# Forming two modulation rows on VectorE in the down-projections of a two-layer step

## The chip, the cores and the metric

The kernel runs on one core of a Trainium2 chip. The metric is the device time of one execution in microseconds (us). Before the change three runs took 1547.54, 1549.52 and 1547.64 us: a median of 1547.64.

## The reference

One step of a small two-layer model on 640 tokens (512 latent, 128 context), with 1024 features. Each layer has a token mixer (neighbourhood attention in layer 0, grouped-query attention in layer 1) and then a gated feed-forward with a convolution of width three. Both stand between normalisations that are scaled, shifted and gated by six modulation rows per layer. A row is a vector of 1024 numbers, once for the latent tokens (from `c`) and once for the context tokens (from `c_ctx`): a matrix product of a single vector with a 1024x1024 part of `ada_w`.

```python
def adaln(cond, w, b):
    m = jax.nn.silu(cond) @ w + b
    return jnp.split(m[..., None, :], 6, axis=-1)

def conv_ffn(h, w_up, conv_w, conv_b, w_down):
    u = h @ w_up
    up = jnp.pad(u, ((0, 0), (1, 1), (0, 0)))
    u = up[:, :-2] * conv_w[0] + up[:, 1:-1] * conv_w[1] + up[:, 2:] * conv_w[2] + conv_b
    a, gt = jnp.split(u, 2, axis=-1)
    return (jax.nn.silu(a) * gt) @ w_down
...
    sh_as, sc_as, g_as, sh_fs, sc_fs, g_fs = adaln(c, ada_w[l], ada_b[l])
...
    xs = xs + g_as * rmsnorm(os_.reshape(bs, ts, -1) @ w_o, norm_mix_post[l])
    hs = rmsnorm(xs, norm_ffn_pre[l]) * (1.0 + sc_fs) + sh_fs
    fs = conv_ffn(hs, ffn_w_up[l], ffn_conv_w[l], ffn_conv_b[l], ffn_w_down[l])
    xs = xs + g_fs * rmsnorm(fs, norm_ffn_post[l])
```

The rows are numbered 0 to 5 in the order of `adaln`'s results: row (l, 2) is the gate of layer l's mixer, row (l, 5) the gate of its feed-forward. A gate row is kept multiplied by the gain of the normalisation that it follows.

## The kernel before

The kernel computes in float32 with matmuls in three passes: each operand is split into a high part (`wh`, `ahi`: a cast on ACT) and a low part (`wl`, `alo`: a difference on DVE or POOL). One helper (L117) records every matmul, so its rows differ only by their tiles.

**Up-projections.** `ffn` (L1155) runs for each layer. Its inner dimension of 2816 is cut into 22 chunks of 128; for each chunk seven block products (`ux`, `uy`, `uz`, 128x322 each) are formed on PE, added up and convolved on ACT and DVE (`C`, `t`, `act`), and the chunk is written to DRAM. Between these block products PE also forms modulation rows (`ada_work`). A row is 8 chunks of contraction, and a chunk four matmuls of `scolp` (the two vectors, 32 columns) with 256 columns of `ada_w` each, which are 8 instructions; several chunks stand together as one group on PE. The last chunk of a row is followed by a sum with the bias on DVE (`arow <- ada, abias`), for some rows by a second operation with the gain, and by two writes to `modrow` in DRAM from ACT's queue. Layer 0 forms five rows there, (0,5), (1,1), (1,0), (1,2), (1,4); layer 1 forms (1,5), at the places that the table `LAST` names, late in the loop.

**Down-projections.** The 640 tokens are five tiles t = 0 to 4. Group 0 holds tiles 0, 1 and 2, group 1 tiles 3 and 4. For each of the 22 chunks k a step loads 512 KB of `w_down` and the chunk's activations by SP, splits them (`load_dn`, four weight buffers), and does six matmuls 128x512 for each tile of the group. `wl` is formed on DVE for even k and on POOL for odd k. Steps 0 to 17 go through all tiles of the group; the last four steps are done tile by tile, so that tile 0 is finished while the others go on. In steps 8, 10, 12 and 14 of group 0 the first four chunks of group 1 are loaded and split ahead (`alo` 128x258 instead of 128x384). The finish of a tile (`Finish`) takes its accumulators, the gate row (`mod`) and the residual (`xo`) through DVE: `xm <- acc,mod`, `xo <- xm,ro,xo`, `xm <- xo,mod`, `xm <- xm,ro,mod`; POOL forms the small factor `ro`. In layer 0 PE then transposes `xm`, and DVE and ACT put the result into `hT`. Tile t's finish in group 0 lies beside the first steps of group 1.

The order of PE is the order of the code. On the other engines a scheduler orders the instructions by their dependences; an engine then works through its queue in that order. Loads by SP and writes from ACT's queue wait in their queues in the same way.

Of the kernel before, what the change touches and what calls it, by code (L numbers as in the profile page):

```python
# [10 lines left out]
F32 = mybir.dt.float32  # L11
# [3 lines left out]
ALU = mybir.AluOpType  # L15
# [4 lines left out]
P = 128  # L20
D = 1024
KC = D // P
# [8 lines left out]
FC = FF // P  # L31
# [30 lines left out]
TP = 1  # L62
PSN = 4
PU0 = 6
LAST = {(10, 6): 1, (8, 6): 3, (5, 6): 3, (1, 6): 3, (1, 5): 1}
HALF = (slice(0, 512), slice(512, D))
DLEAD = 3
DPRE = (8, 10, 12, 14)
# [36 lines left out]
def hybrid_step(ctx: ExitStack, tc: tile.TileContext, A, O):  # L105
    nc = tc.nc
# [9 lines left out]
    def mm(*a, **k):  # L116
        pe(nc.tensor.matmul(*a, **k))  # L117
# [10 lines left out]
    def pool(name, bufs=1, side="left", **k):  # L128
        return tc.tile_pool(name=name, bufs=bufs, side=side, reuse_waits="tile", **k)
# [5 lines left out]
    bk = Banks()  # L135
# [9 lines left out]
    def const_loads():  # L145
# [8 lines left out]
    scolp = cst.tile([P, 2 * KC + 30], F32, name="scolp")  # L154
# [119 lines left out]
    def ada_work(p, rawp, group, steps, todo, wait=1, sizes=()):  # L274

        bias = p.tile([P, 256], F32, name="abias")
        gr = p.tile([P, 256], F32, name="again")
        nc.gpsimd.memset(bias, 0.0)  # L280
        nc.gpsimd.memset(gr, 0.0)

        def quarters(row):
            return row.rearrange("(j c) -> j c", j=4)

        loads = deque((l, idx, k) for l, idx in todo for k in range(KC))
        raws = deque()
# [12 lines left out]
        for _ in range(wait):  # L300
            yield
        sizes = iter(sizes)
        while raws:
            n = min(len(raws), next(sizes, len(raws)))
            for _ in range(n):
                l, idx, k, raw = raws.popleft()
                if k == 0:
                    for q in range(2):
                        nc.sync.dma_start(bias[q::32, :], quarters(A["ada_b"][l, idx * D : idx * D + D]))
                        if idx in gain_of:  # L310
                            nc.sync.dma_start(gr[q::32, :], quarters(A[gain_of[idx]][l]))
# [7 lines left out]
                nc.vector.tensor_add(orow, ps[:, 0:256], bias)  # L319
                bk.put(ps)  # L320
                if idx in gain_of:
                    nc.vector.scalar_tensor_tensor(
                        orow, orow, 1.0 if idx in (1, 4) else 0.0, gr, op0=ALU.add, op1=ALU.mult
                    )
                for q in range(2):
                    nc.scalar.dma_start(quarters(modrow[l][idx][q]), orow[q::32, :])
            for i in range(steps):
                for _ in range(n if steps == 1 else i < n):
                    load()
                yield  # L330

    def drain(gen):
        for _ in gen:
            pass
# [817 lines left out]

    def ffn(l, hT, hT_close, xold, xnew, nxt, todo, late, late_close, side, back, first, fin0, after=None):  # L1155

        s = ExitStack()
        actd = [dr.tile([P, GAP], F32, name=f"act_{l}_{k}") for k in range(FC)]
# [25 lines left out]
        with ExitStack() as s2:  # L1184
# [196 lines left out]
            up = s2.enter_context(pool("up", 2, side))  # L1381
            if todo:
                adap = s2.enter_context(pool("ada", 1, side))
                ada = ada_work(adap, s2.enter_context(pool("adar", 3, side)), 3, *(
                    (8, todo, 4) if nxt else (3, todo, 1, (3, 2, 2, 1))))
            for p in range(PLAIN):
                conv_value(p)
                conv_gate(p)
# [1 line left out]
            for p in range(PLAIN, FC):  # L1390
                nx = p + 1 if p + 1 < FC else None
                for m, q in ((6, p), (5, p), (1, nx), (7, p), (2, nx), (3, p), (4, p)):
                    if q is None:
                        continue
                    evict(m, q, product(m, q))
                    if m == 5:
                        if nx:
                            block_sums(nx)
                        else:
                            lds.append(load_dn(len(lds), *HB[0]))  # L1400
                    elif m == 7:
# [12 lines left out]
                    if ada:  # L1414
                        for _ in range(1 if nxt else LAST.get((FC - p, m), 0)):
                            next(ada, None)
            if ada:
                drain(ada)
            store()
# [7 lines left out]
        fin = Finish(l, 5, xold, xnew, nxt, hTn, xmpool, 5, back)  # L1427
        tail, late, pre = 4, [], deque()
        dn2 = s.enter_context(pool("dn2", 4, side))
        for grp, (c0, c1) in (((0, 1, 2), HB[0]), ((3, 4), HB[1])):  # L1430
            acc = {t: [bk.get("acc") for _ in range(2)] for t in grp}

            def go(t, k, w2, hi, lo, qs=(0, 1)):
                c = (t * P if t < 4 else NS + 1) - c0
                for q in qs:
                    passes(acc[t][q], (hi[:, c : c + P], lo[:, c : c + P]),
                           tuple(x[:, 0, 512 * q : 512 * q + 512] for x in w2), k == 0, k == FC - 1)

            for k in range(FC - tail):
                if len(lds) <= k:  # L1440
                    lds.append(load_dn(k, c0, c1))
                for t in grp:
                    if t != 2 or k >= DLEAD:
                        go(t, k, *lds[k])
                if t == 2 and k == DLEAD - 1:
                    for j in range(DLEAD):
                        go(2, j, *lds[j])
                if t == 2 and k in DPRE:
                    pre.append(load_dn(len(pre), *HB[1], dn2))
                if nxt and late and k in (3, 6):  # L1450
                    late.pop(0)()
            for k in range(FC - tail, FC):
                lds.append(load_dn(k, c0, c1))
            prev, lds, pre = lds, pre, deque()
            for t in grp:
                fin.ahead(t)
                if t == 4 and not nxt:
                    for q in range(2):
                        for i in range(tail):
                            go(t, FC - tail + i, *prev[FC - tail + i], qs=(q,))  # L1460
                    fin.end(t, acc[t][0], acc[t][1], fin.stat(acc[t][0]))
                    continue
# [15 lines left out]
    def gqa_w(c0, u, own=None):  # L1478
# [2 lines left out]
    wkv = []  # L1481
    hT, hp2, late, xmp = ffn(
        0, hT, hp1.close, lambda t: xres[0][t], lambda t: xres[1][t], (1, 1, 0, NS),
        ((0, 5), (1, 1), (1, 0), (1, 2), (1, 4)), late, xmp.close, "right", "left", first, fin,
        lambda u: wkv.append(gqa_w(1024, u)),
    )

# [474 lines left out]
```

## Time and profile before

| | |
|---|---|
| median of three runs | 1547.64 us |
| profiled execution, span of the trace | 1546.0 us |
| PE busy | 1512.8 us |
| DVE, ACT, POOL busy | 1024.1, 854.2, 701.8 us |
| group 0 of layer 0's down-projection | 664.6 to about 755 us |
| group 0 of layer 1's down-projection | 1388.0 to about 1478 us |

Times in rows of the profile are microseconds from the start of the span. A row of a timeline gives start, duration, engine, line, operation, the tile written and the tiles read, their shapes, a count of equal instructions in a row, and in brackets how long the engine was idle ahead of it and what ended that. An instruction's printed time includes the time in which it is held back after its start. A row of a group gives the total busy time and the mean of one in ns. Idle time of an engine costs nothing unless another waits for it, in the end PE.

### The profile page before, as it was taken

To read this page: it belongs to the slowest core of one execution; us is meant where nothing else is said; L and a number is where in the kernel's file an instruction comes from. 1 tells how busy PE (TensorE), PEld (TensorE's weight loads), DVE (VectorE), ACT (ScalarE), POOL (GpSimd) and SP (SyncE) were. 2 spreads that over 40 slices of the span, in tenths; PEclk is the share of its full clock that TensorE was granted. 3 is DMA by queue.
4 is the path that set the end of the run, shared out by engine and by line. 5 is a ranking of instruction groups with operands and counts; after the bars stand their busy time and mean duration, and the time that the engine had idled before them with its cause. 6 is when DMAs were issued, how large, how long until landed. Compare 5 with 4: busy or idle time off the path is not lost.

```text
span 1546.0 us, 26097 instructions
## 1 busy us (share of the span) xinstructions
PE 1512.8 (98%) x9709; PEld 1344.4 (87%) x9709; DVE 1024.1 (66%) x1648; ACT 854.2 (55%) x1624; POOL 701.8 (45%) x606
## 2 busy tenths in 40 slices
PE   6999999999999999999999999999999999999998
PEld 5988998888999999978887878878899999988886
DVE  4553453659877666756757877773988887786554
ACT  5665564646655555654544447763666655554443
POOL 1554463432355455525444464532235666542433
PEclk9999999999999999999999999999999999999999
DMA  9745454253565665388574421015433334447664
GB/s 318 210 122 159 122 132 116 64 190 124 183 224 177 221 190 162 114 277 272 178 234 155 129 69 42 2 40 190 153 114 115 119 111 156 132 164 252 226 221 131
DMA packets 196666, 243.99 MB, mean 158 GB/s; under 512 B 11484, under 2 KB 153020, under 8 KB 196540
## 3 DMA queue, kind: packets, MB, share of 16 engines
q1 hardware_dynamic: 186704, 235.74, 47.7%
q10 hardware_dynamic: 9836, 6.59, 2.5%
q8 instruction: 76, 1.25, 0.3%
q14 instruction: 50, 0.41, 0.1%
HBM read 214.38 MB, written 26.34 MB: 156 GB/s over the span
## 4 chain that ended last, share of the span: by engine, by line
PE 66%; DVE 5%; ACT 2%; issue 2%; POOL 1%; DMA 1%; POOLq 0%; DVEq 0%; ACTq 0%
PE acc L117 19%; PE ux L117 18%; PE uz L117 8%; PE gp L117 5%; PE uy L117 4%; PE po L117 3%; PE y L117 3%; PE s L117 2%; PE tp L120 2%; PE ada L117 1%; DMA wr<-in_ffn_w_up 1%; DVE t L1281 1%; ACT gp L1692 1%; PE tr L120 0%; DVE xo L400 0%
## 5 line engine op out<-in xcount | busy, mean ns | idle before, releaser
L180 POOL TENSOR_TENSOR wl<-wr,wh 128x1024 fp32r<-128x1024 f32 x70 | 173.3, 2480 | 238.5 <-ACT wh L178 223.5
L1204 POOL TENSOR_TENSOR wl<-wr,wh 128x1024 fp32r<-128x1024 f32 x76 | 183.5, 2435 | 46.9 <-ACT wh L1203 43.3
L117 PE MATMUL ux<-B,wh 128*128 128x322 f32 x832 | 200.1, 311 | 0.9 <-ACT u L1258 0.9
L1281 DVE SCALAR_TENSOR_TENSOR t<-C,cw,t 128x644 f32<-128x644 f32 x176 | 156.3, 888 | 51.3 <-ACT t L1279 50.7
L117 PE MATMUL acc<-wh,alo 128*128 128x512 f32 x440 | 172.3, 392 | 0.3 <-DVE alo L1173 0.3
L178 ACT CAST wh<-wr 128x1024 fp32r<-128x1024 f32 x140 | 145.6, 1048 | 48.5 <-DMA wr<-in_ffn_w_down 37.4
L117 PE MATMUL acc<-wh,ahi 128*128 128x512 f32 x440 | 171.9, 391 | 0.0
L117 PE MATMUL acc<-wl,ahi 128*128 128x512 f32 x440 | 171.8, 391 | 0.0
L117 PE MATMUL uz<-B,wh 128*128 128x322 f32 x640 | 156.2, 312 | 0.9 <-ACT v L1258 0.9
L117 PEld LDWEIGHTS ux<-B,wh 128*128 128x128 f32 x832 | 143.6, 189 | 3.4 <-issue 1.2
L1173 DVE TENSOR_TENSOR alo<-ain,ahi 128x384 fp32r<-128x384 f32 (+1 forms) x88 | 84.0, 973 | 84.9 <-ACT ahi L1171 84.0
L117 PE MATMUL ux<-B,wl 128*128 128x322 f32 x416 | 129.5, 311 | 2.7 <-DVE wl L1204 2.7
L117 PE MATMUL qk<-hT,wh 128*128 128x384 f32 (+1 forms) x512 | 122.4, 315 | 0.0
L117 PEld LDWEIGHTS uz<-B,wh 128*128 128x128 f32 x640 | 110.9, 189 | 4.3 <-ACT v L1258 1.5
L1204 POOL TENSOR_TENSOR vl<-wr,vh 128x1024 fp32r<-128x1024 f32 x38 | 96.3, 2535 | 24.6 <-ACT vh L1203 24.3
L1203 ACT CAST wh<-wr 128x1024 fp32r<-128x1024 f32 x84 | 84.8, 1049 | 40.8 <-DVE wr L1227 40.5
L1279 ACT ACTIVATE t<-C,cw 128x644 f32<-128x644 f32 x88 | 78.6, 893 | 47.8 <-DVE C L1309 40.3
L180 DVE TENSOR_TENSOR wl<-wr,wh 128x1024 fp32r<-128x1024 f32 x70 | 91.3, 1315 | 20.1 <-ACT wh L178 19.5
L117 PE MATMUL uz<-B,wl 128*128 128x322 f32 x320 | 99.6, 311 | 0.3 <-POOL wl L1204 0.3
L117 PEld LDWEIGHTS acc<-wh,alo 128*128 128x128 f32 x440 | 82.5, 188 | 18.8 <-DVE alo L1173 1.1
L117 PEld LDWEIGHTS acc<-wl,ahi 128*128 128x128 f32 x440 | 82.6, 188 | 17.9
L117 PEld LDWEIGHTS acc<-wh,ahi 128*128 128x128 f32 x440 | 82.6, 188 | 17.8
(259 smaller groups left out, 3857.7 us busy)
## 6 DMA issues: line engine op xcount, KB each, us to landing
wr<-in_ffn_w_up SPq DMA_DIRECT2D x88, 512.0 KB
wr<-in_ffn_w_down SPq DMA_DIRECT2D x88, 512.0 KB
wr<-in_ada_w SPq DMA_DIRECT2D x72, 512.0 KB
act<-act SPq DMA_DIRECT2D x44, 321.0 KB
wr<-in_na_w_qkv SPq DMA_DIRECT2D x24, 512.0 KB
mod<-modrow SPq DMA_DIRECT2D x20, 512.0 KB
ain<-act SPq DMA_DIRECT2D x44, 192.0 KB
wf<-in_ada_w SPq DMA_DIRECT2D x16, 512.0 KB
```

The lines of the kernel that those rows point to most:

```text
L117: pe(nc.tensor.matmul(*a, **k))
L120: pe(nc.tensor.transpose(*a, **k))
L178: i = nc.scalar.copy(hi, raw)
L180: j = (low or nc.vector).tensor_sub(lo, raw, f32(hi))
L1173: pin(nc.vector.tensor_sub(lo[:, 0 : c1 - c0], ain[:, 0 : c1 - c0], f32(hi[:, 0 : c1 - c0])))
L1203: nc.scalar.copy(hl[0], src)
L1204: low.tensor_sub(hl[1], src, f32(hl[0]))
L1279: nc.scalar.activation(t, taps(0), AF.Identity, bias=cw[:, 3, n : n + 1], scale=cw[:, 1, n : n + 1])
L1281: nc.vector.scalar_tensor_tensor(t, taps(d), cw[:, w, n : n + 1], t, op0=ALU.mult, op1=ALU.add)
L1692: nc.scalar.activation(self.pt[i].rearrange("p (a b) -> p a b", a=2), sv, AF.Exp, bias=nm, scale=-1.0, accum_out=su)
```

## The change

Row (1,2) is no longer formed in layer 0's up-projections, nor row (1,5) in layer 1's, and `LAST` is gone. Layer 1's up-projections hold no modulation work now. A new generator, `ada_vec`, forms the two rows in the down-projections. It takes a row in two halves of 512 columns, and a half in eight units, one for each chunk of contraction. A unit is a load of 256 KB by SP into one of three buffers and two DVE operations 128x512, one for each of the two vectors: a product (`TENSOR_SCALAR`) for the first unit, `raw * scolp + acc` (`SCALAR_TENSOR_TENSOR`) for the others. One step after the eighth unit PE sums `acc` over the partitions: eight matmuls with a column of ones (`one`, 32x128 each, 16 instructions). DVE adds the bias and multiplies by the gain, and ACT's queue writes the half to `modrow`. Layer 1 does a unit in each step of its down-projection, so both halves fall into group 0 (sums over partitions behind steps 8 and 16). Layer 0 does one in each second step: the first half in group 0, the second in group 1.

```diff
+    def ada_vec(p, todo, lag=1):
+        one = p.tile([P, 2, 32], F32, name="one")
...
+        units = deque((l, idx, half, k) for l, idx in todo for half in range(2) for k in range(KC))
...
+                raw = p.tile([P, 512], F32, tag="wr", name="wr", bufs=3)
+                nc.sync.dma_start(raw, A["ada_w"][l, k * P : k * P + P, c0 : c0 + 512])
...
+            if k == 0:
+                acc = p.tile([P, 2, 512], F32, tag="acc", name="acc")
+                for q in range(2):
+                    nc.sync.dma_start(bias[q::32, :], pieces(A["ada_b"][l, idx * D : idx * D + D], half))
+                    if idx in gain_of:
+                        nc.sync.dma_start(gr[q::32, :], pieces(A[gain_of[idx]][l], half))
+            for q in range(2):
+                col = scolp[:, 2 * k + q : 2 * k + q + 1]
+                if k == 0:
+                    nc.vector.tensor_scalar(acc[:, q], raw, col, None, op0=ALU.mult)
+                else:
+                    nc.vector.scalar_tensor_tensor(acc[:, q], raw, col, acc[:, q], op0=ALU.mult, op1=ALU.add)
+            load()
...
+            for _ in range(lag):
+                yield
+            ps = bk.get("ada")
+            for q in range(2):
+                for j in range(4):
+                    mm(ps[32 * j : 32 * j + 32, 0:P], one[:, q], acc[:, q, j * P : j * P + P], start=q == 0, stop=q == 1)
+            nc.vector.tensor_add(bias, ps[:, 0:P], bias)
...
+            for q in range(2):
+                nc.scalar.dma_start(pieces(modrow[l][idx][q], half), bias[q::32, :])
...
-                ada = ada_work(adap, s2.enter_context(pool("adar", 3, side)), 3, *(
-                    (8, todo, 4) if nxt else (3, todo, 1, (3, 2, 2, 1))))
+                ada = ada_work(adap, s2.enter_context(pool("adar", 3, side)), 3, 8, todo, 4)
...
+        vec = ada_vec(s.enter_context(pool("adv", 1, side)), todo_dn)
+        next(vec)
...
+                if not nxt or k % 2:
+                    next(vec, None)
+            if not nxt or t == 4:
+                drain(vec)
...
-        ((0, 5), (1, 1), (1, 0), (1, 2), (1, 4)), late, xmp.close, "right", "left", first, fin,
+        ((0, 5), (1, 1), (1, 0), (1, 4)), ((1, 2),), late, xmp.close, "right", "left", first, fin,
...
-        1, hT, r_h3.close, lambda t: xres[2][t], y_out, None, ((1, 5),), late, xmp.close, "left", "right", first, fin
+        1, hT, r_h3.close, lambda t: xres[2][t], y_out, None, (), ((1, 5),), late, xmp.close, "left", "right", first, fin
```

Line numbers of the changed kernel are 62 higher in `ffn` (L1173 is L1235), and its weight halves stand at L179. PE's order differs only by the groups taken out (in layer 0's up-projections one of 12 matmuls becomes 8, two of 12 and one of 4 go; in layer 1's one of 12, two of 8 and one of 4) and the four groups of eight put in.

DVE at the end of layer 1's up-projection and the start of its down-projection, before:

```order
L1281 SCALAR_TENSOR_TENSOR t<-C,cw_79,t 128x2x322 x4
L319 TENSOR_TENSOR arow<-ada,abias 128x256
L1292 TENSOR_TENSOR act<-t,sl 128x644
L322 SCALAR_TENSOR_TENSOR arow<-arow,again 128x256
L1307 TENSOR_TENSOR C<-ux,v_15534 128x322
L180 TENSOR_TENSOR wl<-wr,wh 128x1024
L1309 TENSOR_TENSOR C<-uz,u_15511 128x322
L1281 SCALAR_TENSOR_TENSOR t<-C,cw_79,t 128x2x322 x2
L1173 TENSOR_TENSOR alo<-ain,ahi 128x384 x3
L1281 SCALAR_TENSOR_TENSOR t<-C,cw_79,t 128x2x322 x2
L1292 TENSOR_TENSOR act<-t,sl 128x644
```

and from the same place in the changed kernel, some rows on (`wl` and the first `alo` are of the first steps):

```order
L1371 TENSOR_TENSOR C<-uz,u_15514 128x322
L1343 SCALAR_TENSOR_TENSOR t<-C,cw_79,t 128x2x322 x2
L1235 TENSOR_TENSOR alo<-ain,ahi 128x384 x2
L372 TENSOR_SCALAR acc<-wr,scolp 128x512 x2
L374 SCALAR_TENSOR_TENSOR acc<-wr,scolp,acc 128x512
L1343 SCALAR_TENSOR_TENSOR t<-C,cw_79,t 128x2x322
L374 SCALAR_TENSOR_TENSOR acc<-wr,scolp,acc 128x512
L1343 SCALAR_TENSOR_TENSOR t<-C,cw_79,t 128x2x322
L374 SCALAR_TENSOR_TENSOR acc<-wr,scolp,acc 128x512
L1354 TENSOR_TENSOR act<-t,sl 128x644
L374 SCALAR_TENSOR_TENSOR acc<-wr,scolp,acc 128x512
L1235 TENSOR_TENSOR alo<-ain,ahi 128x384
```

The two `arow` operations ahead of `C <- ux` are gone, and the units of the moved row stand among the last convolution work and the following `alo`.

DVE in layer 0 where group 0's tile 2 is finished beside group 1's steps 4 to 8, before (`wl` and `alo` at the end are step 8's):

```order
L387 TENSOR_TENSOR xm<-acc,mod 128x512
L389 TENSOR_TENSOR xm<-acc,mod 128x512
L1173 TENSOR_TENSOR alo<-ain,ahi 128x258
L400 SCALAR_TENSOR_TENSOR xo<-xm,ro,xo 128x512 x2
L412 TENSOR_TENSOR xm<-xo,mod 128x512 x2
L419 SCALAR_TENSOR_TENSOR xm<-xm,ro,mod 128x512 x2
L456 TENSOR_TENSOR hT_7811<-tr,hT_7810 128x4x128 x2
L1173 TENSOR_TENSOR alo<-ain,ahi 128x258
L180 TENSOR_TENSOR wl<-wr,wh 128x1024
```

and now:

```order
L451 TENSOR_TENSOR xm<-acc,mod 128x512
L462 SCALAR_TENSOR_TENSOR xo<-xm,ro,xo 128x512 x2
L474 TENSOR_TENSOR xm<-xo,mod 128x512 x2
L481 SCALAR_TENSOR_TENSOR xm<-xm,ro,mod 128x512 x2
L374 SCALAR_TENSOR_TENSOR acc<-wr,scolp,acc 128x512 x5
L518 TENSOR_TENSOR hT_7753<-tr,hT_7752 128x4x128 x2
L374 SCALAR_TENSOR_TENSOR acc<-wr,scolp,acc 128x512 x2
L1235 TENSOR_TENSOR alo<-ain,ahi 128x258
L374 SCALAR_TENSOR_TENSOR acc<-wr,scolp,acc 128x512
L179 TENSOR_TENSOR wl<-wr,wh 128x1024
```

Eight sums of the second half stand between the last operation on tile 2 and step 8's `wl`. The other units of that half (two products and six sums, behind the bias and gain of the first half) stand ahead of tile 0's `xm <- acc,mod`, and the last operation on tile 1 (L481) now stands ahead of step 4's `wl` instead of behind it.

SP in layer 1, the loads around steps 14 and 15 of group 0 (`ain` is the activations, `wr` of `in_ffn_w_down` the weights, 128x258 a preload for group 1), in the changed kernel:

```order
L1231 DMA ain<-act_14_12500 128x384
L173 DMA wr<-in_ffn_w_down 128x1024
L368 DMA again<-in_norm_ffn_post 4x128 x2
L355 DMA wr<-in_ada_w 128x512
L366 DMA abias<-in_ada_b 4x128 x2
L355 DMA wr<-in_ada_w 128x512 x2
L1231 DMA ain<-act_3_12489 128x258
L173 DMA wr<-in_ffn_w_down 128x1024
L355 DMA wr<-in_ada_w 128x512 x2
L1231 DMA ain<-act_15_12501 128x384
```

Before, only `ain` and `wr` of `in_ffn_w_down` alternated there. A unit's load waits until DVE has used the buffer, and the loads behind it in SP's queue wait with it. The load of the gate row for the finish (`mod <- modrow_5`) stood at the start of group 0 and now stands behind the weights of group 1's step 5.

More of the change, by code (lines that the diff above doesn't have):

```diff
@@ L64 @@
 PU0 = 6
-LAST = {(10, 6): 1, (8, 6): 3, (5, 6): 3, (1, 6): 3, (1, 5): 1}
 HALF = (slice(0, 512), slice(512, D))
@@ L330, in ada_work, with pieces, load @@
                 yield
+    def ada_vec(p, todo, lag=1):
+        one = p.tile([P, 2, 32], F32, name="one")
+        nc.gpsimd.memset(one, 0.0)
+        for q in range(2):
+            nc.gpsimd.memset(one[:, q, q : q + 1], 1.0)
+        bias = p.tile([P, P], F32, name="abias")
+        gr = p.tile([P, P], F32, name="again")
+        nc.gpsimd.memset(bias, 0.0)
+        nc.gpsimd.memset(gr, 0.0)
+        def pieces(row, half):
+            return row[512 * half : 512 * half + 512].rearrange("(j c) -> j c", j=4)
+        units = deque((l, idx, half, k) for l, idx in todo for half in range(2) for k in range(KC))
+        raws = deque()
+        def load():
+            if units:
+                l, idx, half, k = units.popleft()
+                c0 = idx * D + 512 * half
+                raw = p.tile([P, 512], F32, tag="wr", name="wr", bufs=3)
+                nc.sync.dma_start(raw, A["ada_w"][l, k * P : k * P + P, c0 : c0 + 512])
+                raws.append((l, idx, half, k, raw))
+        for _ in range(3):
+            load()
+        yield
+        while raws:
+            l, idx, half, k, raw = raws.popleft()
+            if k == 0:
[10 more added lines that the diff above has]
+                    nc.vector.scalar_tensor_tensor(acc[:, q], raw, col, acc[:, q], op0=ALU.mult, op1=ALU.add)
+            load()
+            if k < KC - 1:
+                yield
+                continue
+            for _ in range(lag):
+                yield
+            ps = bk.get("ada")
[3 more added lines that the diff above has]
+            nc.vector.tensor_add(bias, ps[:, 0:P], bias)
+            bk.put(ps)
+            if idx in gain_of:
+                nc.vector.scalar_tensor_tensor(
+                    bias, bias, 1.0 if idx in (1, 4) else 0.0, gr, op0=ALU.add, op1=ALU.mult
+                )
+            for q in range(2):
+                nc.scalar.dma_start(pieces(modrow[l][idx][q], half), bias[q::32, :])
@@ L1150, in hybrid_step, with ffn @@
     r_na.close()
-    def ffn(l, hT, hT_close, xold, xnew, nxt, todo, late, late_close, side, back, first, fin0, after=None):
+    def ffn(l, hT, hT_close, xold, xnew, nxt, todo, todo_dn, late, late_close, side, back, first, fin0, after=None):
         s = ExitStack()
@@ L1414, in ffn @@
                     if ada:
-                        for _ in range(1 if nxt else LAST.get((FC - p, m), 0)):
-                            next(ada, None)
+                        next(ada, None)
             if ada:
```

## The prediction

> **What bounds the kernel now.** I read the page first: the engines' busy shares, the chain that ended last, and the clock.
>
> ```profile
> span 1546.0 us, 26097 instructions
> ...
> PE 1512.8 (98%) x9709; PEld 1344.4 (87%) x9709; DVE 1024.1 (66%) x1648; ACT 854.2 (55%) x1624; POOL 701.8 (45%) x606
> ...
> PEclk9999999999999999999999999999999999999999
> ...
> PE 66%; DVE 5%; ACT 2%; issue 2%; POOL 1%; DMA 1%; POOLq 0%; DVEq 0%; ACTq 0%
> ```
>
> PE is busy for 98% of the span, at full granted clock in every slice, and it makes up 66% of the chain. So a microsecond of PE work taken out is a microsecond gained, as long as nothing behind PE becomes late, and a microsecond that DVE makes PE wait is lost. The question is one of exchange: PE time in the up-projections against DVE time in the down-projections. What PE spends on a modulation group stands in the timeline of layer 1's up-projection (start, duration, instruction, count):
>
> ```profile
> 1286.69 0.31 PE L117 MATMUL ux<-B,wl 128*128 128x322 f32 x1
> 1286.84 0.31 PE L117 MATMUL ux<-B,wh 128*128 128x322 f32 x1
> 1287.07 1.50 PE L117 MATMUL ada<-wr,scolp 128*32 128x256 f32 x24
> 1288.51 0.41 PE L117 MATMUL uz<-B,wh 128*128 128x322 f32 x1
> 1288.76 0.31 PE L117 MATMUL uz<-B,wl 128*128 128x322 f32 x1
> ...
> 1380.00 0.64 PE L117 MATMUL ada<-wr,scolp 128*32 128x256 f32 x8
> ```
>
> Block matmuls start 0.15 us apart (1286.69, 1286.84). From 1286.84 to 1288.76 would be 0.30 without the group and is 1.92, so 24 instructions cost **1.62 us**, 0.12 more than their printed 1.50. With the same 0.12, 8 cost 0.76; each instruction is (1.50 - 0.64)/16 = 0.054, so 16 cost 1.62 - 8 x 0.054 = 1.19.
>
> **What the change takes away.** A row is 64 PE instructions. Layer 1's row stands as 24, 16, 16 and 8: 1.62 + 1.19 + 1.19 + 0.76 = **-4.76**. In layer 0 the order of PE loses two groups of 24, one of 8, and 8 instructions of another: 1.62 + 1.62 + 0.76 + 8 x 0.054 = **-4.43**.
>
> At the end of layer 1's up-projection DVE and ACT lose work as well, first DVE:
>
> ```profile
> 1384.19 0.42 DVE L319 TENSOR_TENSOR arow<-ada,abias 128x256 f32<-128x256 f32 x1
> 1384.52 0.82 DVE L1292 TENSOR_TENSOR act<-t,sl 128x644 f32<-128x644 f32 x1
> 1385.26 0.41 DVE L322 SCALAR_TENSOR_TENSOR arow<-arow,again 128x256 f32<-128x256 f32 x1
> 1385.59 0.48 DVE L1307 TENSOR_TENSOR C<-ux,v 128x322 f32<-128x322 f32 x1
> ```
>
> and next to it on PE, then on ACT:
>
> ```profile
> 1386.13 0.42 PE L117 MATMUL ux<-B,ah 128*128 128x322 f32 x1 [1.23 <-DVE C L1307]
> ```
>
> ```profile
> 1386.78 0.51 ACT L1171 CAST ahi<-ain 128x384 fp32r<-128x384 f32 x1 [3.02 <-DMA modrow<-arow]
> ```
>
> PE waits 1.23 us there for C, which stood behind both row operations. Without them C is about 2 x 0.33 us earlier (starts 1385.26 to 1385.59). The next activations of ACT stood behind a wait of 3.02 us for the row's write, and with it goes a short wait of PE for the second step's operands. What is late next is DVE's own queue of convolution work, so I take **-1.0**, between 0 and -1.4. The row that now ends layer 0's up-projection ends as before, so nothing goes there.
>
> **What it adds on PE.** Four groups of 16 matmul instructions with half the columns (32x128). No row shows that shape. If time follows columns they take 0.33 + 16 x 0.027 = 0.76, if it follows instructions 1.19; I take 0.8, nearest to the columns that the 322 and 512 wide rows follow: **+3.2** (3.0 to 4.8). The POOL memsets and the small loads of bias and gain lie in idle time: POOL waited 8.56 us before its first weight half of the down-projection.
>
> ```profile
> 1388.38 2.41 POOL L180 TENSOR_TENSOR wl<-wr,wh 128x1024 fp32r<-128x1024 f32 x1 [8.56 <-ACT wh L178]
> ```
>
> **What it adds on DVE.** Per row 28 three-operand sums and 4 products of 128x512. The nearest rows by form:
>
> ```profile
> L400 DVE SCALAR_TENSOR_TENSOR xo<-xm,ro,xo 128x512 f32<-128x512 f32 x40 | 28.4, 746 | 4.8 <-POOL ro L379 3.9 <-DMA xo<-in_x_sample 0.8
> L597 DVE TENSOR_SCALAR xT<-xT,gcol,hcol 128x512 f32<-128x512 f32 x8 | 4.3, 543 | 2.1 <-ACT hT L596 2.0
> ```
>
> The same sum takes 0.75 alone and 1.41 for two in a row (771.01 below), the product 0.54. A unit is 1.4 us, a row about 22 us of DVE. DVE can afford that on average; what counts is where it stands.
>
> **Layer 0, group 1.** The order puts six sums and two products ahead of the finish of tile 0, and eight sums between the last operation of tile 2 (771.01) and the weight half of step 8 (773.88).
>
> ```profile
> 744.30 0.69 DVE L387 TENSOR_TENSOR xm<-acc,mod 128x512 f32<-128x512 f32 x1 [4.60 <-ACT junk L370]
> ...
> 756.83 5.69 DVE L419 SCALAR_TENSOR_TENSOR xm<-xm,ro,mod 128x512 f32<-128x512 f32 x2 [1.08 <-POOL ro L379]
> ...
> 771.01 1.41 DVE L419 SCALAR_TENSOR_TENSOR xm<-xm,ro,mod 128x512 f32<-128x512 f32 x2 [1.09 <-POOL ro L379]
> ...
> 773.88 1.22 DVE L180 TENSOR_TENSOR wl<-wr,wh 128x1024 fp32r<-128x1024 f32 x1
> 775.01 2.96 DVE L1173 TENSOR_TENSOR alo<-ain,ahi 128x258 fp32r<-128x258 f32 x2
> ```
>
> and on POOL, then on PE, at the same times:
>
> ```profile
> 756.76 5.21 POOL L180 TENSOR_TENSOR wl<-wr,wh 128x1024 fp32r<-128x1024 f32 x2
> ...
> 774.75 2.60 POOL L180 TENSOR_TENSOR wl<-wr,wh 128x1024 fp32r<-128x1024 f32 x1 [3.78 <-ACT wh L178]
> ```
>
> ```profile
> 779.77 0.40 PE L117 MATMUL acc<-wh,ahi 128*128 128x512 f32 x1
> 780.00 0.39 PE L117 MATMUL acc<-wl,ahi 128*128 128x512 f32 x1
> ```
>
> The first part (6 x 0.7 + 2 x 0.54 = 5.3 us) mostly fills the 4.60 us idle; the load for its third unit is issued late, and DVE's wait of 1.08 ahead of 756.83 takes up part of that, so tile 2 comes about 1 us late (0 to 2.5). The second part adds 8 x 0.67 = 5.4. And POOL's own half (774.75) now falls among these sums: where two such operations meet, one waits for the other. Two sums took 5.69 us at 756.83 instead of 1.41 while POOL worked from 756.76 to 761.97, and two alo took 2.96 at 775.01 instead of 0.8. So one block more, 2.3. Against that stands the slack: the half of step 8 ends at 775.1, and PE uses it at 780.00, or 0.8 later for the ones ahead: 5.7. Stall: 1 + 5.4 + 2.3 - 5.7 = **+3.0**, between 0 (no block, no lateness) and 6.3 (a second block and the full lateness).
>
> A rule bears on the block. The Trainium skill, "SBUF — State Buffer", section "Who interferes with whom", says that a DVE instruction with two SBUF inputs and a GpSimd instruction that reads SBUF share a port as an exclusive lock: the second waits for the whole of the first. It speaks against this change, as every added sum has two SBUF inputs. The rows at 756.83 and 775.01 agree. By it the term is 3.0 as above; without it the block of 2.3 would go and 0.7 remain.
>
> **Layer 1, group 0.** Here there is a unit in every step. A step is 18 matmuls 0.23 us apart (779.77 to 780.00): 4.1 us. Two steps, 8.2 us, hold on DVE two alo, one weight half and now four sums, and one weight half on POOL:
>
> ```profile
> 1410.94 0.55 DVE L1173 TENSOR_TENSOR alo<-ain,ahi 128x384 fp32r<-128x384 f32 x1
> ```
>
> The busy table by stretch (PE, PEld, DVE, ACT, POOL busy, clock, DMA share, GB/s) has for 20 us of it:
>
> ```profile
> 1400.00:1420.00 20.00, 20.00 (x90) 16.57 (x89) 13.29 (x13) 11.68 (x18) 7.81 (x4) 1.00 0.80 266
> ```
>
> For two steps that is 1.1 + 1.2 + 2.8 = 5.1 on DVE, blocked once by POOL's 2.4: 7.5 of 8.2. The 13.29 that DVE shows now hold blocked time too. The preloads for group 1 add four short alo, two halves on each engine: 1.6 + 2.4 + 4.8 = 8.8 us. Eight steps that hold them need 4 x 7.5 + 8.8 = 38.8 us of 32.9 if nothing overlaps: 5.9 too much, which a lead of 3 to 6 us over PE from the steps ahead has to cover. I take **+1.5**, between 0 and 5.9. Layer 0's group 0 has a unit in every second step: 0 (to 1).
>
> **Sum.** -4.76 - 4.43 - 1.0 + 3.2 + 3.0 + 1.5 = -2.5. From the span of 1546.0 this gives 1543.5. The runs' median of 1547.64 is 1.64 above that span; with this it is **1545.2**.
>
> **Rivals.** *The stalls vanish* (the leads are enough): -4.76 - 4.43 - 1.0 + 3.2 + about 1 = -6.0, **1541.6**. For it: DVE is at 66%, and buffers run ahead. Against it: eight sums in one piece ahead of a weight half.
>
> *DVE and POOL become the bound* (the slower side): neither stretch has the lead, so layer 0 pays 6.3 and layer 1 5.9: -10.2 + 3.2 + 12.2 = +5.2, **1552.9**. It decides against the change once the two stalls together pass 7.0 + 3.1 us. For it: the rows above, where DVE and POOL exclude each other. Against it: DVE was idle for 4.60 us ahead of 744.30, and for 1.1 twice after.
>
> *Loads become the bound in layer 1*. A unit of 0.26 MB in 4.1 us is 64 GB/s more, 330 where 266 stood at a share of 0.80, so about 1.0 of the engines; SP issues unit loads that wait for DVE with weight loads queued behind them.
>
> ```profile
> 1426.53 1.05 ACT L178 CAST wh<-wr 128x1024 fp32r<-128x1024 f32 x1 [6.53 <-DMA wr<-in_ffn_w_down]
> ```
>
> Casts already wait for weights. From 1400 to 1420 the free share is 0.20 x 20 = 4.0 us, and five units, 1.3 MB at 266/0.80 = 333 GB/s, need 3.9; if bursts leave half of it unused, 2 us are missing, on top of the 1.5: **1547.2**, and the weights behind that queue late.
>
> *The removal gives less than it says*: the groups covered waits for evictions or weights, and PE now waits for those instead. Half of 9.2 lost: **1549.8**. Against it: no wait is printed behind the groups above.
>
> *Layer 1's gate row is late*: its last sums end with step 16, and tile 0's finish reads it back after step 17 and four tail steps of six matmuls, 4.1 + 5.5 = 9.6 us later. The chain is two DVE operations (0.8), a write (3.02, the wait of ACT above) and a read, taken as long: about 7 us, and what stands ahead of it in the queues. 2 us late gives **1547.2**.
>
> **How the numbers follow.** 0.2% is about what a measurement of this kernel can tell from no change: 3.1 us, 1544.5 to 1550.7. Chances: forecast 0.36 (own range 1543.5 to 1548), stalls vanish 0.27, DVE and POOL bound 0.15, loads 0.12, less removed 0.06, late gate row 0.04. Faster: 0.27 and a quarter of the forecast, 0.36. Slower: 0.15 and small parts of loads and removal, 0.19. Same: 0.45. The range for 8 in 10 reaches from 1540.8, near the sum without stalls, to 1551.5, into the case of the bound; beyond it lie the lowest of the first and the half of the second.
>
> **What will show it.** The up-projections should lose the groups named, PE's wait of 1.23 at 1386 should be shorter, and ones groups of about 0.65 printed should stand in four places. Layer 0's step 8 should show PE waiting 1 to 6 us for wl or alo. In layer 1 PE's waits up to step 17 should sum to under 6 us, named DVE if the lock is right, DMA if the loads are. No wait in step 8 of layer 0, or single waits above 5 us elsewhere, make this wrong.

## The result and the profile after

The changed kernel took 1559.53 us (median of 5 runs, 1558.4 to 1560.91) against 1547.64 us: a ratio of 1.0076, 95% interval 1.0065 to 1.0087. It is **slower by 11.9 us** (0.8%), outside the range of 1540.8 to 1551.5 that was forecast. The profiled run has a span of 1556.6 us, 10.6 more than before. Its page:

```profile
span 1556.6 us, 26097 instructions
...
PE 1512.1 (97%) x9645; PEld 1343.5 (86%) x9645; DVE 1077.7 (69%) x1716; ACT 853.5 (55%) x1624; POOL 705.5 (45%) x614
...
PE 35%; DVE 4%; ACT 2%; DMA 2%; issue 2%; POOL 1%; SPq 0%; DVEq 0%; POOLq 0%; ACTq 0%
```

PE's share of the last chain fell from 66% to 35%: at some point the chain now leaves PE. PE's busy time hardly fell, although 64 instructions net are gone; that will matter below. What PE waited for, from the view of waits (engine, tile and line, releaser: total us, times, longest):

```profile
PE acc L116 <- DVE wl L179: 3.8, 1, 3.8
...
PE acc L116 <- DVE act L1354: 3.3, 2, 1.6
...
PE acc L116 <- POOL wl L179: 2.4, 2, 1.5
...
PE tr L119 <- DVE hT L518: 1.2, 1, 1.2
```

None of the four stood in the profile before. To see how much each stage gained or lost, the same PE instruction is looked up in both timelines: a matmul at the start of each down-projection, and the first long wait of the stage after layer 0's. Before:

```profile
668.19 0.50 PE L117 MATMUL acc<-wh,alo 128*128 128x512 f32 x1 [0.27 <-DVE alo L1173]
...
824.39 0.73 PE L117 MATMUL gp<-wl,hT 128*128 128x512 f32 x2 [0.39 <-DVE wl L180]
...
1391.41 0.50 PE L117 MATMUL acc<-wh,alo 128*128 128x512 f32 x1
```

and after:

```profile
662.98 0.50 PE L116 MATMUL acc<-wh,alo 128*128 128x512 f32 x1 [0.27 <-DVE alo L1235]
...
831.33 0.73 PE L116 MATMUL gp<-wl,hT 128*128 128x512 f32 x2 [0.41 <-DVE wl L179]
...
1395.39 0.50 PE L116 MATMUL acc<-wh,alo 128*128 128x512 f32 x1 [0.27 <-DVE alo L1235]
```

Up to layer 0's down-projection the changed kernel is 5.2 us ahead, of which 0.7 is the wait for the first load of the program (7.4 us against 8.1). At the end of that down-projection it is 6.9 behind: **12.1 us lost there**. Up to layer 1's down-projection it catches up to 4.0 behind, a gain of 3.0; layer 1's mixer, which did not change, takes about 0.5 of that stretch's gain. At the end it is 10.6 behind: **6.6 lost** in layer 1's down-projection.

Where the 12.1 went: PE at step 8 of layer 0's group 1 shows the largest part.

```profile
779.27 0.40 PE L116 MATMUL acc<-wh,ahi 128*128 128x512 f32 x1
783.47 0.80 PE L116 MATMUL acc<-wl,ahi 128*128 128x512 f32 x1 [3.80 <-DVE wl L179]
784.06 0.63 PE L116 MATMUL acc<-wh,alo 128*128 128x512 f32 x1
...
788.75 0.58 PE L116 MATMUL acc<-wl,ahi 128*128 128x512 f32 x1
789.17 0.39 PE L116 MATMUL acc<-wh,alo 128*128 128x512 f32 x1
```

After the wait of 3.80 us the matmuls start 0.43 us apart instead of 0.23, up to 788.75. The busy table of these 10 us shows why:

```profile
780.00:790.00 10.00, 6.53 (x17) 5.16 (x18) 8.59 (x13) 2.81 (x4) 2.37 (x1) 0.66 0.59 197
```

The granted clock, the share of its full clock that PE was given, is 0.66 over this stretch (third number from the end). The page, whose slices are 39 us long, shows 9 in every one. From 783.47 to 789.17 thirteen matmuls take 5.70 us where 13 x 0.233 = 3.03 would do: **2.7 us on top of the wait**. Slow matmuls count as busy, and that is one reason why PE's busy time hardly fell; the groups of ones are another. The Trainium skill, "TensorE: Matmul & The Clock Gate", "Part 1: The HAM clock gate", says that TensorE falls to half clock after an idle window of about 3.4 us and comes back after a busy one. The wait of 3.80 us here agrees; runs below show a fall behind shorter waits too.

The DVE queue ahead of that half, and POOL beside it:

```profile
771.88 1.42 DVE L481 SCALAR_TENSOR_TENSOR xm<-xm,ro,mod 128x512 f32<-128x512 f32 x2 [1.09 <-POOL ro L441]
773.22 5.54 DVE L374 SCALAR_TENSOR_TENSOR acc<-wr,scolp,acc 128x512 f32<-128x512 f32 x5
778.68 1.27 DVE L518 TENSOR_TENSOR hT<-tr,hT 128x512 fp32r<-128x512 f32 x2
779.88 1.39 DVE L374 SCALAR_TENSOR_TENSOR acc<-wr,scolp,acc 128x512 f32<-128x512 f32 x2
781.20 0.41 DVE L1235 TENSOR_TENSOR alo<-ain,ahi 128x258 fp32r<-128x258 f32 x1
781.54 0.73 DVE L374 SCALAR_TENSOR_TENSOR acc<-wr,scolp,acc 128x512 f32<-128x512 f32 x1
782.20 1.21 DVE L179 TENSOR_TENSOR wl<-wr,wh 128x1024 fp32r<-128x1024 f32 x1
```

```profile
774.26 2.62 POOL L179 TENSOR_TENSOR wl<-wr,wh 128x1024 fp32r<-128x1024 f32 x1 [2.41 <-ACT wh L177]
```

Tile 2 is 0.87 us late (771.88 against 771.01), the eight sums stand where the order has them, and five of them take 5.54 us instead of 3.4 while POOL forms its half. All eight take 5.54 + 1.39 + 0.73 = 7.66 us; the prediction had 5.4 + 2.3. What it had differently is the place of PE. It let PE come 0.8 us later, for the ones. PE came 0.5 us earlier than before (779.27 against 779.77 for the matmul ahead of the wait), because the gain of the up-projections was not yet used up. That is 1.3 us less slack, and more than the whole difference between 3.0 and 3.80.

What it did not have is the wait for `act`. DVE at the start of layer 0's down-projection:

```profile
664.72 0.89 DVE L372 TENSOR_SCALAR acc<-wr,scolp 128x512 f32<-128x512 f32 x2 [1.32 <-DMA wr<-in_ada_w]
665.52 0.55 DVE L1235 TENSOR_TENSOR alo<-ain,ahi 128x384 fp32r<-128x384 f32 x1
665.99 0.88 DVE L1343 SCALAR_TENSOR_TENSOR t<-C,cw,t 128x644 f32<-128x644 f32 x1
666.78 0.74 DVE L374 SCALAR_TENSOR_TENSOR acc<-wr,scolp,acc 128x512 f32<-128x512 f32 x1
667.44 0.88 DVE L1343 SCALAR_TENSOR_TENSOR t<-C,cw,t 128x644 f32<-128x644 f32 x1
668.24 0.74 DVE L374 SCALAR_TENSOR_TENSOR acc<-wr,scolp,acc 128x512 f32<-128x512 f32 x1
668.90 0.82 DVE L1354 TENSOR_TENSOR act<-t,sl 128x644 f32<-128x644 f32 x1
```

The first product waits 1.32 us at the head of the queue for its load, and two sums stand ahead of the last `act`. `act` reads `t`, which lies in PSUM, the memory of PE's accumulators, and tile 2's accumulators take its place there. So PE waits for it at the first matmul of tile 2, 1.61 us in layer 0 and 1.65 in layer 1:

```profile
669.87 0.47 PE L116 MATMUL acc<-wh,ahi 128*128 128x512 f32 x1 [1.61 <-DVE act L1354]
```

POOL has no part in this wait. Its last work ahead of it ends at 661.99, and its next half comes behind it:

```profile
674.20 2.73 POOL L179 TENSOR_TENSOR wl<-wr,wh 128x1024 fp32r<-128x1024 f32 x1 [12.21 <-ACT wh L177]
```

So layer 0's 12.1 are the waits of 1.61, 1.25 and 3.80, 2.7 of slow clock and two groups of ones (0.78 each, below), 10.9. Layer 1's 6.6 are waits of 1.65, 0.88 and 1.49 and two groups of ones, 5.6. Part of the 2.2 left over lies around the waits: the three matmuls at 667.87, 669.87 and 670.18 take 2.31 us from the first start to the last instead of 0.46, so the wait printed as 1.61 costs 1.85.

### The profile page after: what moved, and what is told of

The parts are those of the page before. It is cut to its first block, busy times and chain, and to the rows that moved or that the text cites. A ratio compares the mean times of both kernels' runs of the same rounds, so it can differ in the third digit from the quotient of the medians.

```text
span 1556.6 us, 26097 instructions
## 1 busy us (share of the span) xinstructions
PE 1512.1 (97%) x9645; PEld 1343.5 (86%) x9645; DVE 1077.7 (69%) x1716; ACT 853.5 (55%) x1624; POOL 705.5 (45%) x614
## 3 DMA queue, kind: packets, MB, share of 16 engines
q8 instruction: 76, 1.25, 0.3%
## 5 line engine op out<-in xcount | busy, mean ns | idle before, releaser
L179 POOL TENSOR_TENSOR wl<-wr,wh 128x1024 fp32r<-128x1024 f32 x70 | 174.5, 2496 | 250.8 <-ACT wh L177 246.0
L1235 DVE TENSOR_TENSOR alo<-ain,ahi 128x258 fp32r<-128x258 f32 (+1 forms) x88 | 74.8, 867 | 61.5 <-ACT ahi L1233 55.7
L1265 ACT CAST wh<-wr 128x1024 fp32r<-128x1024 f32 x84 | 84.7, 1049 | 46.5 <-DVE wr L1289 46.2
L1233 ACT CAST ahi<-ain 128x258 fp32r<-128x258 f32 (+1 forms) x88 | 39.5, 460 | 120.8 <-PE acc L116 79.7
L179 DVE TENSOR_TENSOR wl<-wr,wh 128x1024 fp32r<-128x1024 f32 x70 | 92.7, 1335 | 15.7 <-ACT wh L177 15.1
```

Of the source, the lines that this page charges most:

```text
L179: j = (low or nc.vector).tensor_sub(lo, raw, f32(hi))
L1233: pin(nc.scalar.copy(hi[:, 0 : c1 - c0], ain[:, 0 : c1 - c0]))
L1235: pin(nc.vector.tensor_sub(lo[:, 0 : c1 - c0], ain[:, 0 : c1 - c0], f32(hi[:, 0 : c1 - c0])))
L1265: nc.scalar.copy(hl[0], src)
```

## The experiments

Three theories stood open. **Place**: sums push back a few DVE operations that PE waits for. **Loads**: the extra loads crowd the DMA engines and SP. **Throughput or lock**: DVE and POOL together have too much to do, because they exclude each other, so that one stands still while the other works. The runs of one group share runs of the kernel before on the same chip (1548.0 to 1548.5 us); ratios are to those.

**One row at a time, and parts left out.** Layer 0's row alone, with layer 1's back in its up-projection:

```diff
-        1, hT, r_h3.close, ..., None, (), ((1, 5),), late, ...
+        1, hT, r_h3.close, ..., None, ((1, 5),), (), late, ...
```

> Only layer 0's row (1,2) is moved; layer 1's row (1,5) is formed in its up-projection as before. Place theory (the sums push back DVE operations that PE waits for, act ahead of tile 2's accumulators and the weight half of step 8, and PE then runs at half clock for some us): layer 0 gives 4.4 us and loses 12, so about 7.5 us slower than before, 1555. Load theory (the extra loads crowd the DMA engines and SP's queue): layer 0 adds its loads at half the rate of layer 1 and should carry less than half of the 11.9 us lost, so 1550 or less.

Measured 1556.47, ratio 1.0065 (1.0047 to 1.0083): 8.5 us slower. The waits are 1.37, 1.25 and 3.79 us at the same places, and the clock falls again. The smaller load rate costs more, which speaks against loads. In its profiled run, the slowest of the four (1561.38 us), layer 1 waited 2.73 us for a POOL half though nothing is added there. So layer 1 has little to spare even without the added sums, in this execution at least.

Layer 1's row alone:

```diff
-        ((0, 5), (1, 1), (1, 0), (1, 4)), ((1, 2),), late, ...
+        ((0, 5), (1, 1), (1, 0), (1, 2), (1, 4)), (), late, ...
```

> Only layer 1's row (1,5) is moved. Place theory: its up-projection gives about 3.9 us, its down-projection loses 7 (tile 2's start 2, two weight halves of POOL 3.4, two ones groups 1.5), so 3 us slower than before, 1550.7. Load theory: the larger part of the 11.9 us, 1554 or more.

Measured 1549.22, ratio 1.0006 (0.9996 to 1.0015): no difference that can be told, against 3 us expected from the place theory and 6 or more from loads. Its waits in layer 1 are the one for `act` (1.18) and four of 0.2 to 0.5. Both rows apart cost 8.5 + 1.2 = 9.7 us, near the 11.9 of both together.

DVE's operations cut to 8 of 512 columns, everything else kept:

```diff
-    nc.vector.scalar_tensor_tensor(acc[:, q], raw, col, acc[:, q], op0=ALU.mult, op1=ALU.add)
+    nc.vector.scalar_tensor_tensor(acc[:, q, 0:8], raw[:, 0:8], col, acc[:, q, 0:8], op0=ALU.mult, op1=ALU.add)
```

> Both rows moved with all their loads and sums over partitions, but the operations on VectorE work on 8 of 512 columns, so the two rows are wrong. Place theory: the waits in both down-projections are gone, the time is 8.3 us below before plus 3 us for the ones groups plus about 1 for what is left, 1543. Load theory: the waits stay, 1555 or more.

Measured 1542.85, ratio 0.9967 (0.9956 to 0.9978): every wait that the change brought into the two down-projections is gone. Loads, groups of ones and writes are all still there. **The loads by themselves cost nothing; the loss comes with DVE's sums.**

The rows not formed at all; of `ada_vec` only the writes are left, and they write zeros:

```diff
-            for q in range(2):
-                col = scolp[:, 2 * k + q : 2 * k + q + 1]
...
+                for q in range(2):
+                    nc.scalar.dma_start(pieces(modrow[l][idx][q], half), bias[q::32, :])
```

> The two rows are not formed at all: no loads, no sums, no ones groups, only the writes of zeros to the rows' place. This is what the removal gives by itself. The prediction's terms: 4.76 + 4.43 + 1.0 = 10.2 us, 1537.4. Cover theory (in layer 1 the groups taken out covered waits of PE for ACT's evictions, of which the changed kernel shows 0.95 and 0.72 us): about 8.3 us, 1539.3.

Measured 1541.06, ratio 0.996 (0.9945 to 0.9975): taking the rows out of the up-projections gives 7.0 us (3.9 to 8.5 by the interval), not the 10.2 of the prediction; the 8.3 of the cover theory is still within. Layer 1's PE shows where some of it stays:

```profile
1370.57 0.41 PE L116 MATMUL uz<-B,wl 128*128 128x322 f32 x1 [0.56 <-POOL wl L1238]
...
1373.41 0.41 PE L116 MATMUL ux<-B,wh 128*128 128x322 f32 x1 [0.96 <-ACT u L1292]
...
1376.20 0.42 PE L116 MATMUL uz<-B,wh 128*128 128x322 f32 x1 [0.73 <-ACT v L1292]
```

The wait of 1.23 for `C` is gone, and three of 2.25 together stand in its place: the last modulation group covered them, in part. Instead of -1.0 the transition is +0.8 (2.25 less the 1.23 and 0.20 that stood there before). The changed kernel shows the same three places, with 0.44, 0.94 and 0.72: +0.7.

**Moving the sums.** First unit held behind the last `act`, by an order without a wait:

```diff
+        marks["hold"] = marks["act"]
...
+                if marks.get("hold"):
+                    behind(i, marks["hold"])
```

> The changed kernel with the first unit's product held behind the last act operation of the up-projection on VectorE (an order without a wait, in both layers). Place theory: act is no longer late, tile 2's accumulators are free in time, and the waits of 1.61 and 1.64 us at step 2 of both down-projections go: 1559.5 - 3.3 = 1556. Throughput theory (VectorE and GpSimd together have too much to do, wherever it stands): the same work is only later, the waits come back at the following weight halves: 1559.

Measured 1555.79, ratio 1.0052 (1.0038 to 1.0065), as the place theory has it in time, but not quite in its parts: both waits for `act` are gone, while layer 1 now waits 3.34 us once for a DVE half instead of 0.88 and 1.49 for POOL's. There the throughput theory is right. The profiled run is the slowest of its four (1558.16 us); it also pays for a slow clock in layer 0's up-projection, shown in the last section.

The last four units of layer 0's row held behind the low parts of steps 9 to 15:

```diff
+                marks["hold"] = marks["alo"] if nxt and grp[0] == 3 and k >= 9 else None
-                if not nxt or k % 2:
+                if not nxt or (k % 2 and (grp[0] == 0 or k != 7)):
```

> The changed kernel with the last four units of layer 0's row held behind the activations' low part of steps 9, 11, 13 and 15 of group 1, so that the eight sums no longer stand ahead of step 8's weight half. Place theory: the wait of 3.80 us goes, and with it the half clock that follows it (6.8 us at half speed, 3.4 us): 1559.5 - 7.2 = 1552. Throughput theory: the wait moves to steps 10 to 16 and most of the loss stays, 1557 or more.

Measured 1551.3, ratio 1.0021 (1.0012 to 1.003): 8.2 us less than the changed kernel. The wait at step 8 is gone, and the clock stays at full speed.

Only the last two units held back:

```diff
+                marks["hold"] = marks["alo"] if nxt and grp[0] == 3 and k >= 11 else None
```

> The changed kernel with only the last two units of layer 0's row held back (four sums instead of eight ahead of step 8's weight half). Dose test of the half clock: the wait should shrink by 4 x 0.68 = 2.7 us to about 1.1 us. If the half clock follows only a long wait (it followed 2.73 and 3.80 us, and none of the waits up to 1.65), it goes too: 1559.5 - 2.7 - 3.4 = 1553.4. If it follows any wait at this place: 1556.8.

Measured 1553.76, ratio 1.0034 (1.0021 to 1.0048). The wait at step 8 is 1.13 us, and the matmuls behind it keep their pace:

```profile
782.86 0.50 PE L116 MATMUL acc<-wl,ahi 128*128 128x512 f32 x1 [1.13 <-DVE wl L179]
783.20 0.40 PE L116 MATMUL acc<-wh,alo 128*128 128x512 f32 x1
```

2.7 us less of waiting gave 5.8 us by the medians: behind the short wait the price of the slow clock is not paid.

Both holds:

> Both holds of the two runs above together. Place theory: 1559.5 - 3.3 - 7.2 = 1549, about level with before (1548.0), and what is left against the run without rows (1541.1) is four ones groups (3.0), layer 1's late weight halves (2 to 3) and layer 0's transposes (1 to 2). Throughput theory: 1556 or more.

Measured 1549.37, ratio 1.0006 (0.9997 to 1.0015): level with before, with the loss at step 8 and at `act` gone. What is left is mainly a wait of 2.38 us in layer 1 (the clock is 0.83 over those 10 us) and 1.26 ahead of layer 0's transposes. DVE and POOL ahead of the first:

```profile
1433.53 10.50 DVE L376 SCALAR_TENSOR_TENSOR acc<-wr,scolp,acc 128x512 f32<-128x512 f32 x6
```

```profile
1431.36 7.33 POOL L179 TENSOR_TENSOR wl<-wr,wh 128x1024 fp32r<-128x1024 f32 x2 [5.98 <-ACT wh L177]
1440.15 2.68 POOL L179 TENSOR_TENSOR wl<-wr,wh 128x1024 fp32r<-128x1024 f32 x1 [1.46 <-ACT wh L177]
```

Six sums that need 4.0 us take 10.50, and the first two halves of POOL, which need 4.8, take 7.33. The two engines take turns. Looked at one by one, three of the six sums take 2.88 to 2.90 us and three 0.73 or 0.74, one long sum for each of the three halves. So a half on POOL costs DVE about 2.2 us of standing still, more than the 1.2 it needs to form the half itself.

**Taking POOL out of the pair.** All weight halves of the down-projections on DVE:

```diff
-            w2 = wsplit(rows(w_dn, k, 1, 0, D), 1, D, nc.gpsimd if k % 2 else None, own)
+            w2 = wsplit(rows(w_dn, k, 1, 0, D), 1, D, None, own)
```

With both holds:

> The run with both holds, and the weight halves of odd steps of the down-projections formed on VectorE instead of GpSimd. Lock theory (two operations of 128x1024 and 128x512 on GpSimd and VectorE with two inputs in SBUF exclude each other, so a half on GpSimd costs VectorE about 2.3 us of standing still, more than the 1.22 us of doing it itself): the wait of 2.38 us in layer 1 and its 1.7 us of half clock and the 1.26 us ahead of layer 0's transposes go: 1549.4 - 5 = 1544.5, faster than before (1548.5). Load theory of VectorE (no lock, its queue is simply full): 1.22 us more in every second step, 1553 or more.

Measured 1542.06, ratio 0.9963 (0.995 to 0.9975): 7.3 us less than with the holds alone, and no wait of PE in either down-projection. The kernel before with this edit alone:

> The kernel before with the same one edit: odd weight halves of the down-projections on VectorE. PE waits nowhere there on them, so by both theories nothing changes: 1548 to 1549. If it is faster by 2 us or more, the gain of the run with both holds is not the lock's beside the sums.

Measured 1546.88, ratio 0.9995 (0.9986 to 1.0004): nothing, although there too DVE stands still less (its `alo` groups take 46.2 us instead of 84.2). PE waited on none of it. The changed kernel with this edit and no hold:

> The changed kernel with the same one edit and no hold (five sums, not eight, then stand ahead of step 8's weight half, by the scheduler). Lock theory: the wait at step 8 falls below 2 us and the half clock goes, layer 1's late halves go, the waits for act stay: 1559.5 - 3 - 3.4 - 2.4 = 1551. Load theory: 1562 or more.

Measured 1542.6, ratio 0.9968 (0.9956 to 0.998): **17 us less than the changed kernel, from more work on DVE**, as good as with the holds, and 8 less than the 1551 expected. PE waits for nothing in either down-projection. DVE's groups by form in the changed kernel (total us, mean ns):

```profile
L179 DVE TENSOR_TENSOR wl<-wr,wh 128x1024 fp32r<-128x1024 f32 x70 | 92.7, 1335 | 15.7 <-ACT wh L177 15.1
...
L374 DVE SCALAR_TENSOR_TENSOR acc<-wr,scolp,acc 128x512 f32<-128x512 f32 x56 | 54.2, 1009 | 2.2 <-DMA wr<-in_ada_w 2.2
L1235 DVE TENSOR_TENSOR alo<-ain,ahi 128x384 fp32r<-128x384 f32 x44 | 45.3, 1037 | 23.7 <-ACT ahi L1233 18.0 <-DMA wr<-in_ada_w 5.6
L1235 DVE TENSOR_TENSOR alo<-ain,ahi 128x258 fp32r<-128x258 f32 x44 | 30.3, 696 | 37.8 <-ACT ahi L1233 37.8
```

and with the halves on DVE:

```profile
L179 DVE TENSOR_TENSOR wl<-wr,wh 128x1024 fp32r<-128x1024 f32 x114 | 143.1, 1263 | 26.8 <-ACT wh L177 25.6 <-DMA ain<-act 0.8
...
L374 DVE SCALAR_TENSOR_TENSOR acc<-wr,scolp,acc 128x512 f32<-128x512 f32 x56 | 39.8, 750 | 3.0 <-DMA wr<-in_ada_w 3.0
L1235 DVE TENSOR_TENSOR alo<-ain,ahi 128x384 fp32r<-128x384 f32 x44 | 28.0, 638 | 25.4 <-ACT ahi L1233 25.3
L1235 DVE TENSOR_TENSOR alo<-ain,ahi 128x258 fp32r<-128x258 f32 x44 | 18.8, 427 | 20.8 <-ACT ahi L1233 20.8
```

The same 144 operations take 86.6 us instead of 129.8: 43 us in which DVE stood still behind POOL are gone. The 44 halves that it now forms itself cost 50 us (114 take 143.1 us, the 70 of the changed kernel 92.7), so its queue carries about the same total. But no operation is held back at a bad moment for a whole half of POOL, and PE no longer waits for POOL's slower half.

The edit changed the order on DVE as well; the expectation had that for step 8, not for the start. The scheduler moved three of the eight sums behind step 8's half. At the start of layer 0's down-projection the first product no longer waits for its load, one sum instead of two stands ahead of the last `act`, and `act` starts 3.75 us after the matmul that was looked up in the timelines above (661.95 here) instead of 5.92; before it was 3.05. That wait went by order alone, since POOL had no part in it. The run with both holds got a new order too: the six sums above stand there in pairs, with halves between them. So the lengths show the pairing and its price for DVE, but how much of the 17 us, or of the 7.3, comes from the pairing and how much from the order stays open. That it is a port of SBUF, the memory of the tiles, on which the two meet is what the Trainium skill says ("SBUF — State Buffer", "Who interferes with whom"); the runs do not show the port.

## Why the prediction was wrong

The forecast of the span was 1543.5 us and the profiled run has 1556.6, 13.1 more. **The step that failed is the price of what DVE makes PE wait.** The prediction had stalls of 3.0 and 1.5 at two places, nothing at the others, and nothing for the clock. The runs show waits of 10.7 us at six places and 2.7 us of slow clock behind one of them, 8.9 more than the 4.5. Layer 1's transition, which was given the wrong sign, makes 1.7. The remaining 2.5 are small parts whose cause stays open. Term by term:

- **The removal from the up-projections**, -9.2 on PE: right in layer 0 (5.2 us ahead, less 0.7 of the first load). The **transition of layer 1**, -1.0, was wrong: "what is late next is DVE's own queue" was named and priced at nothing, and the waits on ACT and POOL that the last group covered came out, +0.7 in the changed kernel and +0.8 in the run without rows. The rival "the removal gives less than it says" holds for this part: 7.0 instead of 10.2 altogether.
- **The four groups of ones**, 3.2: right. In the trace a group takes 0.65 printed, and 0.78 with the gaps around it (the matmuls at 735.00, 735.89 and 736.24 take 1.24 instead of 0.46 us).
- **Layer 0, group 1**, 3.0: the step was right in place, in the length of the sums and with one block by POOL, which the rows show directly (5.54 for 3.4). The wait measured 3.80, because PE came 0.5 us earlier and not 0.8 later. Two things beside it were missing: the transposes waited 1.25 for `hT` (PE was still 2.1 us ahead of before there, and DVE 0.9 behind: 765.46 against 764.59 for `hT`), and the wait itself cost 2.7 more through the clock. The sentence that failed is "a microsecond that DVE makes PE wait is lost": here 3.80 cost 6.5.
- **The start of both down-projections**, 0 in the prediction: the order rows in front of it show the sums ahead of `act`, and `act` was not followed to what it sets free. 1.61 and 1.65.
- **Layer 1, group 0**, 1.5 within 0 to 5.9: within its bounds, at 0.88 + 1.49 = 2.4, and up to 3.34 when the start is repaired. The lead that was to cover the 38.8 us of work for 32.9 was taken a little too large.
- The rival "DVE and POOL become the bound" had the mechanism for its two places, at 0.15, and is nearest in time (1552.9). At those places the waits are 3.80, 0.88 and 1.49, with the transposes' 1.25 7.4 us, short of the 10.1 at which it was to decide. The slow clock and the waits for `act`, which it does not have, took the loss past that.
- The other rivals: loads are excluded as the cause by the run with thin sums; the late gate row of layer 1 shows nowhere in PE's waits.

With the stalls gone the rest of the sum holds: -9.2 + 0.8 + 3.2 = -5.2, and the changed kernel with all halves on DVE measures 5.5 us less than the kernel before.

## What to carry to other kernels

Ahead of moving work to VectorE, add up its time together with GpSimd's wherever both have operations that read two tensors from SBUF. Here they took turns, and a half that GpSimd formed in 2.4 us cost VectorE more than forming it in 1.2. Follow every operation that the new work is put ahead of to what it sets free, PSUM among it. Where a change makes TensorE gain time early, subtract that gain from the slack of everything that comes later. And price a wait of TensorE longer than some 1.5 to 2 us at its length plus the slow clock that may follow it; here that added up to 2.7 us.

## What the runs showed of the hardware

In the down-projections the granted clock fell behind waits of PE of 2.38, 2.73, 2.74, 3.34 and 3.80 us, and not behind those up to 1.65 us. Behind 3.80 the table over 10 us shows 0.66, behind the other four it shows 0.83, half as much lost. The Trainium skill, "TensorE: Matmul & The Clock Gate", "Part 1: The HAM clock gate", gives an idle window of about 3.4 us for this; here waits a good deal shorter were enough, and the measurement decides.

But there is no sharp limit of length. In layer 0's up-projection the run with the first unit held has a wait of 1.86 us and half clock behind it, and the run with two units held has 1.84 us at the same place and full clock. Each PE row is followed by the table of a microsecond behind it, first the run with the first unit held:

```profile
371.85 0.42 PE L116 MATMUL ux<-B,wl 128*128 128x322 f32 x1 [1.86 <-DVE wl L1271]
```

```profile
374.00:375.00 1.00, 1.00 (x5) 1.00 (x5) 1.00 (x2) 0.43 (x1) 0.00 (x0) 0.50 0.97 290
```

and the run with two units held:

```profile
373.25 0.42 PE L116 MATMUL ux<-B,wl 128*128 128x322 f32 x1 [1.84 <-DVE wl L1271]
```

```profile
374.00:375.00 1.00, 1.00 (x9) 1.00 (x8) 1.00 (x3) 0.83 (x1) 0.00 (x0) 1.00 0.39 114
```

At the program's start, where PE works in short bursts, a wait of 1.54 us is followed by half clock in the run without rows and by full clock in the kernel before. So the length of a wait does not decide alone. What else decides was not tested.

The best version here is the changed kernel with the weight halves of the down-projections on VectorE: 1542.6 us, and 1542.06 with both holds, 5.5 and 6.1 us below the kernel before.
